# Between two attention layers: weight splits moved from VectorE and GpSimd to ScalarE and GpSimd, masked values written directly, PSUM banks taken one at a time

## The chip, the cores and the metric

The kernel runs on one core of a Trainium2 chip. The time is the device time of one execution in microseconds (us). Of the engines, TensorE (PE) multiplies matrices, VectorE (DVE), ScalarE (ACT) and GpSimd (POOL) work element by element, and SyncE (SP) issues most of the transfers. Each engine works through its own instructions in the order in which they are written; semaphores tie the engines together.

## The reference

Two layers, each `x <- x + RMSNorm_post(Mixer(RMSNorm_pre(x)))`, for 512 tokens of 1,024 columns in float32. Layer 0 is sparse attention with 16 heads in 4 groups: compressed keys and values (blocks of 32 tokens through a small network), selected blocks and a window, mixed by gates. Layer 1 is differential attention with 8 heads. Cut to what matters here:

```
u = rmsnorm(x, norm_pre[0]);  q, kc, vc, ks, vs, kw, vw, gate, z = split(u @ w_in)
o_c = softmax(q @ k_cmp + bias) @ v_cmp          # 31 compressed blocks per group
o   = gate0*o_c + gate1*o_s + gate2*o_w
x   = x + rmsnorm((o * silu(z)) @ w_out, norm_post[0])
u = rmsnorm(x, norm_pre[1]);  q, k, v, z = split(u @ dw_in)
a = softmax(q1 @ k1) - lam * softmax(q2 @ k2)    # differential attention, then a @ v
```

## The kernel before

**Splitting.** A float32 operand is split into two parts, a rounded high one (`hi`, names ending in h, whi) and the rest (`lo`, names ending in l, wlo), and a product is three matmuls: high by high, low by high, high by low. Weights are loaded (`wraw`, or for a few pieces two `P` tiles) and split piece by piece by `Stream.split`: a copy makes the high part (L163 ACT, L165 POOL, or for one piece L159), a subtraction the low part (L167, or L160). A piece listed in `ws.by` is split by the engines that a table names, two letters for each quarter: first the engine of the high part, then that of the low part (A = ScalarE, P = GpSimd, D = VectorE). `SPD` is the table of the first piece of `dv1`; its split parts lie in the tiles `wx`.

**Jobs.** A projection is a job whose function `run` yields after each step of three matmuls. Layer 0 ends with the jobs oA, oB, oC and `o1` (output projection, second half of its columns, four token tiles t = 0 to 3, matmuls at L467). Layer 1 begins with `dv0` and `dv1`, the value projections (`tjob`, matmuls at L218, results copied out at L571 by ACT). `dv0` goes token tile by token tile.

**The seam between the layers.** When a token tile of `o1` is done, its row sum of squares is taken (L453 ACT), the product with the norm's weights (L454 DVE), the inverse root (L345 ACT, L346 to L352 DVE) and the new x (`bigD`, L1052 DVE, two halves). `prenorm` then takes the sum of squares of the new x (L361 ACT), multiplies x by the next norm's weights (L364 POOL, two halves, into `bigC`), computes a root again (L345 to L349), scales `bigC` (L369 DVE, two halves) and returns `turn`: eight transposes by PE (L380) into two PSUM tiles T, whose high part ACT writes (L100, into `bigF`) and whose low part DVE writes (L105, into `bigE`). `bigF` and `bigE` are the operands of layer 1's projections. `T["pre", t]()` is the turn of tile t, called p0 to p3 here; the string `SEQ` writes the order on PE out by hand: a0 to a3 are the token tiles of `dv0` (24 matmuls each), b0 to b3 those of the first half of `dv1` (12 each).

**PSUM.** `bank(tag)` takes a bank of 128 x 512: 2 with tag mm, 2 with S, 3 with T, 1 with av. The rest of the order is set by a scheduler that simulates the program and by the pools' buffers; only PE's order in the seam is fixed.

**Compressed values.** Class `Cmp`, one for each group: `t` turns the probabilities and prepares the value operand `vt`: for each of four heads the same 64 columns, multiplied by that head's mask (`bmask`, one column each, so that rows of other heads are zero), split in two. Before, DVE writes the masked copy with one instruction (L918, into a P tile), ACT rounds it (L100) and DVE subtracts (L105 PT<-P). `v` multiplies (L931 to L933) and adds into the output (L935). L870 and L878 are the product of probabilities with values and its sum into the output.

Of the kernel before, what the change touches and what calls it, by code (L numbers as in the profile page):

```python
# [21 lines left out]
PRE1 = 29  # L22
# [20 lines left out]
SPD = ('PD',)*4  # L43
SEQ = 'a0 a1 p2 b0 b1 a2 p3 b2 a3 b3'.split()
# [24 lines left out]
def trunk(ctx: ExitStack, tc: tile.TileContext, x, table, npre, npost, w_in, pe_k, w1_k, w2_k,  # L69
# [135 lines left out]
    def tjob(name, w, width, col, n, evac, banks, cuts=((0, 4), (4, 4)), by_token=False):  # L205
        def run(i):
            bs = [bank(b) for b in banks]
            per = 4 // len(bs)
            acc = [bs[t // per][:, (t % per) * n:(t % per) * n + n] for t in range(NT)]
# [14 lines left out]
            if by_token:  # L224
                for ci in range(len(cuts)):
                    cut[ci] = ws.cut.pop(i + ci)
                for t in range(NT):
                    for ci in range(len(cuts)):
                        yield from part(ci, t)
                    evac(t, acc[t])  # L230
                for _ in cuts:
                    if i:
                        ws.split()
                return
# [120 lines left out]
    def prenorm(t, src, xn, grow, uh, ul, early):  # L355
# [6 lines left out]
        if early:  # L362
            for c, g in zip(halves, grow):
                nc.gpsimd.tensor_tensor(xn[:, c], src[:, c], g, op=OP.mult)  # L364
# [226 lines left out]
    for n in range(4):  # L591
        tjob(f"dv{n}", dw_in, DIFF_IN, 2048 + n * 256, 256, evac_dv(n), (("S", "S"), ("mm", "mm"))[n % 2],
             by_token=n == 0)
# [287 lines left out]
    class Cmp:  # L881
# [22 lines left out]
        def t(self, i):  # L904
            g = self.g
            if True:
                p = bank("T")
                for qb in range(NT):
# [7 lines left out]
                vb = ptile()  # L916
                v3 = vb[:, 0:256].rearrange("p (h d) -> p h d", h=4)
                nc.vector.tensor_tensor(v3, T["vc"][:, g:g + 1, :].to_broadcast([128, 4, 64]),  # L918
                                        bmask[:, :, None].to_broadcast([128, 4, 64]), op=OP.mult)
                vt = pttile()  # L920
                hi(vt[:, 0:256], vb[:, 0:256])
                lo(vt[:, 256:512], vb[:, 0:256], vt[:, 0:256])
# [156 lines left out]
    with tc.manual_schedule(engines={mybir.EngineType.PE}):  # L1079
        run.upto("oC")  # L1080
        while run.i <= index["o1"]:
            run.step()
            if run.done - T.setdefault("o1b", run.done) > PRE1 * 640:
                if ("pre", 1) in T:
                    T.pop(("pre", 1))()
# [4 lines left out]
        for w in SEQ:  # L1090
            if w[0] == "p":
                T["pre", int(w[1])]()
            else:
                for _ in range({"a": 8, "b": 4}[w[0]]):
                    next(gens["ab".index(w[0])], None)
        for g in gens:
            for _ in g:
                pass
# [180 lines left out]
```

## Time and profile before

| what | value |
|---|---|
| runs | 663.24, 663.30, 665.05 us; median 663.3 us |
| profiled execution, its own time | 661.7 us |
| its span, first to last instruction | 659.8 us |
| PE busy | 635.3 us of the span |
| granted TensorE clock, mean | 0.99 of full speed |

The profiled execution lies 1.6 us below the median of the others; differences are worked out against it and then taken from the median. A PE that is busy for 96% of the span leaves about 24.5 us in which it does nothing, and some of those are the start and the end.

### The profile page before, as it was taken

Reading aid. Unit: us, or ns where it says so; the run is one execution under the profiler, and the core shown is the slowest. Engines: PE = TensorE matmul, PEld = TensorE weight load, DVE = VectorE, ACT = ScalarE, POOL = GpSimd, SP = SyncE. Lnnn points to the kernel's source line nnn. Section 1 sums busy time; section 2 is a strip of 40 time slices with the busy share of each in tenths; the row PEclk is TensorE's granted clock in tenths of the full one; section 3 lists DMA queues with packets and bytes.
Section 4 is the critical chain, followed back from the end, with each engine's and each line's share of the span. In section 5 each row is a group of like instructions: output and inputs, shape, how many; then the busy total and the mean of one; then the engine's idle time right before and its main releaser. Section 6 shows DMA issues by size and latency. Waiting matters only on the chain.

```text
span 659.8 us, 11242 instructions
## 1 busy us (share of the span) xinstructions
PE 635.3 (96%) x3773; PEld 555.5 (84%) x3773; DVE 413.7 (63%) x1188; ACT 340.3 (52%) x904; POOL 401.3 (61%) x675
## 2 busy tenths in 40 slices
PE   6999999999999999999999899999999998989996
PEld 5888888888788788888887899898987987879885
DVE  5611235678778978969878900236558668797634
ACT  6311234675767567768564311235564574668431
POOL 4778558777777587768586457948674563522300
PEclk8999999999999999999999899999999998999998
DMA  8565423213022111201852212322333232225302
GB/s 254 145 166 132 124 76 92 60 34 71 27 65 66 33 47 41 58 17 36 298 187 96 96 54 75 117 74 89 88 81 79 68 80 62 65 64 191 129 25 103
DMA packets 68989, 60.52 MB, mean 92 GB/s; under 512 B 3628, under 2 KB 60868, under 8 KB 68932
## 3 DMA queue, kind: packets, MB, share of 16 engines
q1 hardware_dynamic: 68212, 57.45, 29.9%
q10 hardware_dynamic: 720, 2.36, 0.9%
q8 instruction: 30, 0.49, 0.3%
q14 instruction: 27, 0.22, 0.1%
HBM read 55.04 MB, written 4.76 MB: 91 GB/s over the span
## 4 chain that ended last, share of the span: by engine, by line
PE 81%; DVE 11%; ACT 3%; DMA 3%; issue 2%; POOL 0%; SPq 0%; DVEq 0%; ACTq 0%; POOLq 0%
PE mm L198 31%; PE mm L218 12%; PE mm L467 6%; PE T L856 5%; PE av L870 5%; PE S L218 5%; PE S L801 4%; PE S L800 4%; PE S L467 3%; PE av L1166 2%; PE T L721 1%; DMA wraw<-in_nsa_w_in_dram 1%; PE T L1156 1%; DMA P<-in_nsa_w_out_dram 1%; DVE P L792 1%
## 5 line engine op out<-in xcount | busy, mean ns | idle before, releaser
L167 POOL TENSOR_TENSOR wlo<-wraw,whi 128x256 fp32r<-128x256 f32 (+2 forms) x247 | 184.2, 774 | 23.8 <-ACT whi L163 12.4
L165 POOL TENSOR_SCALAR whi<-wraw 128x256 fp32r<-128x256 f32 (+1 forms) x240 | 95.5, 424 | 111.9 <-PE mm L198 65.9
L794 ACT ACTIVATE P<-P,st 128x512 f32<-128x512 f32 (+3 forms) x192 | 107.5, 560 | 87.6 <-DVE st L792 86.7
L850 POOL TENSOR_SCALAR P<-P,st,gate 128x512 f32<-128x512 f32 (+3 forms) x128 | 80.1, 637 | 27.0 <-DVE st L847 24.9
L792 DVE CUSTOM_DVE_ANT_0 P<-S,BT 128x128 f32<-128x128 f32 (+2 forms) x144 | 59.7, 418 | 28.6 <-PE S L801 26.1
L198 PE MATMUL mm<-bigA,whi 128*128 128x512 f32 x192 | 77.4, 403 | 0.1
L198 PE MATMUL mm<-bigA,wlo 128*128 128x512 f32 x192 | 75.3, 392 | 0.0
L198 PE MATMUL mm<-bigB,whi 128*128 128x512 f32 x192 | 75.3, 392 | 0.0
L105 DVE TENSOR_TENSOR PT<-T,PT 128x512 fp32r<-128x512 f32 x84 | 56.9, 685 | 8.2 <-ACT PT L100 6.4
L870 PE MATMUL av<-PT,bigE 128*128 128x512 f32 x160 | 56.4, 417 | 1.2 <-DVE bigF L878 0.9
L105 DVE TENSOR_TENSOR stk<-mm,stk 64x512 fp32r<-64x512 f32 x32 | 22.0, 688 | 52.5 <-ACT stk L100 52.1
L198 PE MATMUL mm<-bigF,whi 128*128 128x512 f32 x128 | 51.9, 405 | 0.0
L856 PE MATMUL T<-ident,P 128*128 128x128 f32 x320 | 51.8, 272 | 0.0
L100 ACT ACTIVATE PT<-T 128x512 fp32r<-128x512 f32 x84 | 48.6, 592 | 6.0 <-PE T L856 3.9
L856 PEld LDWEIGHTS T<-ident,P 128*128 128x128 f32 x320 | 41.0, 140 | 12.3 <-issue 0.4
L100 ACT ACTIVATE stk<-mm 64x512 fp32r<-64x512 f32 x64 | 37.8, 591 | 25.8 <-PE mm L198 14.9
L198 PE MATMUL mm<-bigE,whi 128*128 128x512 f32 x128 | 50.8, 397 | 0.0
L198 PE MATMUL mm<-bigF,wlo 128*128 128x512 f32 x128 | 50.7, 396 | 0.0
L218 PE MATMUL mm<-whi,bigF 128*128 128x256 f32 x176 | 50.3, 287 | 0.1
L218 PE MATMUL mm<-wlo,bigF 128*128 128x256 f32 x176 | 50.0, 285 | 0.0
L218 PE MATMUL mm<-whi,bigE 128*128 128x256 f32 x176 | 49.6, 283 | 0.0
L198 PEld LDWEIGHTS mm<-bigB,whi 128*128 128x128 f32 x192 | 36.1, 188 | 8.1
(288 smaller groups left out, 1650.8 us busy)
## 6 DMA issues: line engine op xcount, KB each, us to landing
wraw<-in_diff_w_in_dram SPq DMA_DIRECT2D x31, 512.0 KB, 3.9
wraw<-in_nsa_w_in_dram SPq DMA_DIRECT2D x26, 512.0 KB, 4.1
BT<-rd SPq DMA_DIRECT2D x32, 128.0 KB, 3.4
wraw<-in_diff_w_out_dram SPq DMA_DIRECT2D x5, 512.0 KB, 4.0
bigF<-in_x_dram SPq DMA_DIRECT2D x4, 512.0 KB, 9.5
wraw<-in_nsa_w_out_dram SPq DMA_DIRECT2D x4, 512.0 KB, 3.4
bigD<-in_x_dram SPq DMA_DIRECT2D x4, 512.0 KB, 3.7
x1d<-bigD ACTq DMA_DIRECT2D x4, 512.0 KB, 4.9
```

Of the source, the lines that this page charges most:

```text
L100: return nc.scalar.activation(dst, src, AF.Copy, scale=scale)
L105: nc.vector.tensor_tensor(dst, src, h.bitcast(F32), op=OP.subtract)
L165: nc.gpsimd.tensor_scalar(h[:, a:b], v, 1.0, 0.0, op0=OP.mult, op1=OP.add)
L167: e.tensor_tensor(l[:, a:b], v, h[:, a:b].bitcast(F32), op=OP.subtract)
L198: T["mm"] = nc.tensor.matmul(p[:, a:b], wt[:, k, :], u[:, k, a:b], start=(k == 0 and j == 0), stop=(k == KD - 1 and j == 2)).ins
L218: nc.tensor.matmul(acc[t], u[:, k0 + k, t * 128:(t + 1) * 128], wt[:, k, :], start=(ci == 0 and k == 0 and j == 0 and t % per == 0), stop= ...
L467: nc.tensor.matmul(p, U[u][:, k, t * 128:(t + 1) * 128], wt[wi], start=start and j == 0, stop=stop and j == 2, skip_group_check=True)
L792: nc.vector.tensor_tensor_reduce(out=o, in0=i0, in1=b, op0=OP.add, op1=OP.min, scale=-1.0, scalar=BIG, accum_out=nm)
L794: nc.scalar.activation(pt[:, :n], pt[:, :n], AF.Exp, bias=nm, scale=-1.0, accum_out=den)
L850: NORM(nc, i, br, qb).tensor_scalar(self.P[i][:, :n], self.P[i][:, :n], st[:, 8 + i:9 + i], gate[:, NT - 1 - qb, c:c + 1], op0=OP.mult, op ...
L856: T["tmark"] = nc.tensor.transpose(p[:, j * 128:(j + 1) * 128], self.P[j][:, kb * 128:(kb + 1) * 128], ident).ins
L870: nc.tensor.matmul(av, T["V"][:, br, kb, g, :], p, start=(br == 0 and kb == 0 and j == 0), stop=(br == 1 and kb == qb and j == 1))
```

## The change

Five edits, the first four at the seam. (1) The four quarters of the first piece of `dv1` get their high part from ScalarE and their low part from GpSimd, instead of GpSimd and VectorE. (2) The turn p1 is called after `o1` instead of after 29 of its steps, so behind its last three matmuls. (3) `dv0` takes a PSUM bank for each token tile when it comes to it, with the tags S, T, S, S, instead of two S banks, two token tiles in each, before it starts. (4) What the seam's block issues on POOL stays behind the last L364 instruction (`issue_after`). (5) `Cmp.t` writes no masked copy: for each head ACT writes the high part with the mask as its scale, and DVE computes value times mask minus the high part.

```
-PRE1 = 29
-SPD = ('PD',)*4
-SEQ = 'a0 a1 p2 b0 b1 a2 p3 b2 a3 b3'.split()
+SPD = ('AP',)*4
+SEQ = 'p1 a0 a1 p2 b0 b1 a2 p3 b2 a3 b3'.split()
...
-            bs = [bank(b) for b in banks]
-            per = 4 // len(bs)
-            acc = [bs[t // per][:, (t % per) * n:(t % per) * n + n] for t in range(NT)]
+            if by_token:
+                per, acc = 1, [None] * NT
+            else:
+                bs = [bank(b) for b in banks]
+                per = 4 // len(bs)
+                acc = [bs[t // per][:, (t % per) * n:(t % per) * n + n] for t in range(NT)]
...
                 for t in range(NT):
+                    acc[t] = bank(banks[t])[:, :n]
                     for ci in range(len(cuts)):
...
-                nc.gpsimd.tensor_tensor(xn[:, c], src[:, c], g, op=OP.mult)
+                T["xm"] = nc.gpsimd.tensor_tensor(xn[:, c], src[:, c], g, op=OP.mult).ins
...
-        tjob(f"dv{n}", dw_in, DIFF_IN, 2048 + n * 256, 256, evac_dv(n), (("S", "S"), ("mm", "mm"))[n % 2],
-             by_token=n == 0)
+        tjob(f"dv{n}", dw_in, DIFF_IN, 2048 + n * 256, 256, evac_dv(n),
+             (("S", "T", "S", "S"), ("mm", "mm"), ("S", "S"), ("mm", "mm"))[n], by_token=n == 0)
...
-                vb = ptile()
-                v3 = vb[:, 0:256].rearrange("p (h d) -> p h d", h=4)
-                nc.vector.tensor_tensor(v3, T["vc"][:, g:g + 1, :].to_broadcast([128, 4, 64]),
-                                        bmask[:, :, None].to_broadcast([128, 4, 64]), op=OP.mult)
                 vt = pttile()
-                hi(vt[:, 0:256], vb[:, 0:256])
-                lo(vt[:, 256:512], vb[:, 0:256], vt[:, 0:256])
+                for h in range(4):
+                    a, b, m = vt[:, 64 * h:64 * h + 64], vt[:, 256 + 64 * h:320 + 64 * h], bmask[:, h:h + 1]
+                    hi(a, T["vc"][:, g], m)
+                    nc.vector.scalar_tensor_tensor(b, T["vc"][:, g], m, a.bitcast(F32), op0=OP.mult, op1=OP.subtract)
...
-        while run.i <= index["o1"]:
-            run.step()
-            if run.done - T.setdefault("o1b", run.done) > PRE1 * 640:
-                if ("pre", 1) in T:
-                    T.pop(("pre", 1))()
+        run.upto("o1")
...
+        with tc.issue_after(T["xm"]):
+            for w in SEQ:
...
```

How the instructions stand now, at three places. The line numbers of the change differ by one to three: L159 there is L160 of before, L164 is L165, L166 is L167, L220 is L218, L351 is L348, L367 is L364, L383 is L380, L470 is L467, L795 is L792, L850 is L847 and L881 is L878; L923 is the new subtraction.

PE at the end of `o1` (tile t = 3, the S bank), before:

```order
L467 MATMUL S<-wx,bigA 128x512 x2
L467 MATMUL S<-wx,bigB 128x512
L380 MATMUL T<-ident,bigC 128x128 x8
L467 MATMUL S<-wx,bigA 128x512 x2
L467 MATMUL S<-wx,bigB 128x512
L218 MATMUL S<-whi,bigF 128x256
L218 MATMUL S<-wlo,bigF 128x256
```

and in the change:

```order
L470 MATMUL S<-wx,bigA 128x512 x2
L470 MATMUL S<-wx,bigB 128x512
L470 MATMUL S<-wx,bigA 128x512 x2
L470 MATMUL S<-wx,bigB 128x512
L383 MATMUL T<-ident,bigC 128x128 x8
L220 MATMUL S<-whi,bigF 128x256
L220 MATMUL S<-wlo,bigF 128x256
```

The eight transposes of p1 moved behind the last three matmuls of `o1`.

POOL in the seam, before; the four L364 instructions are tiles 0 and 1, then tiles 2 and 3:

```order
L364 TENSOR_TENSOR bigC<-bigD,P 128x512 x4
L165 TENSOR_SCALAR whi<-wraw 128x256 x4
L167 TENSOR_TENSOR wlo<-wraw,whi 128x256 x2
L159 TENSOR_SCALAR wx<-P 128x256 x4
L167 TENSOR_TENSOR wlo<-wraw,whi 128x256 x2
L364 TENSOR_TENSOR bigC<-bigD,P 128x512 x4
L165 TENSOR_SCALAR whi<-wraw 128x256 x4
```

and in the change:

```order
L367 TENSOR_TENSOR bigC<-bigD,P 128x512 x4
L159 TENSOR_TENSOR wx<-P,wx 128x256 x4
L367 TENSOR_TENSOR bigC<-bigD,P 128x512 x4
L164 TENSOR_SCALAR whi<-wraw 128x256 x4
L166 TENSOR_TENSOR wlo<-wraw,whi 128x256 x4
L164 TENSOR_SCALAR whi<-wraw 128x256 x4
```

Between tiles 1 and 2 four subtractions stand where twelve instructions stood; eight of those (the second piece of `dv1`) went behind tile 3, and the four copies (before's L159) went to ACT, where they stand ahead of tile 2's L361.

DVE around the compressed values of the second group, before:

```order
L792 ISA st 128x1
L918 TENSOR_TENSOR P<-vcmp,bmask 128x256
L878 TENSOR_TENSOR bigF<-av,PT 64x2x128 x2
L105 TENSOR_TENSOR PT<-T,PT 128x512
L792 ISA P,st<-S,BT_78 128x512
```

and in the change, some ten rows further on:

```order
L850 RECIPROCAL st<-st 128x2
L104 TENSOR_TENSOR PT<-T,PT 128x512
L923 SCALAR_TENSOR_TENSOR PT<-vcmp,bmask,PT 128x64 x4
L795 ISA P,st<-S,BT_78 128x512
L795 ISA st 128x1
L881 TENSOR_TENSOR bigF<-av,PT 64x2x128 x2
```

The masked product is gone from in front of the sum L878, and four small subtractions stand where one of 256 columns stood.

## Rows read from the trace of the kernel before

**Rows 1.** The page's first part: busy us, share of the span, instructions of each engine.
```profile
PE 635.3 (96%) x3773; PEld 555.5 (84%) x3773; DVE 413.7 (63%) x1188; ACT 340.3 (52%) x904; POOL 401.3 (61%) x675
```
**Rows 2.** Waits of PE over the span: us in total, times, longest.
```profile
PE av L870 <- DVE bigF L878: 0.9, 1, 0.9
```
**Rows 3.** Timeline of PE: start, duration (us), instruction, [idle before <- releaser].
```profile
359.02 0.39 PE L467 MATMUL S<-wx,bigB 128*128 128x512 f32 x1
...
362.42 1.25 PE L380 MATMUL T<-ident,bigC 128*128 128x128 f32 x8 [0.97 <-DVE bigC L369]
363.43 0.71 PE L467 MATMUL S<-wx,bigA 128*128 128x512 f32 x2
...
364.21 0.28 PE L218 MATMUL S<-whi,bigF 128*128 128x256 f32 x1
...
366.97 0.28 PE L218 MATMUL S<-whi,bigE 128*128 128x256 f32 x1
369.69 0.58 PE L218 MATMUL S<-whi,bigF 128*128 128x256 f32 x1 [2.44 <-ACT bigA L571]
...
374.09 1.04 PE L380 MATMUL T<-ident,bigC 128*128 128x128 f32 x8
```
**Rows 4.** Timeline of DVE in the same stretch.
```profile
357.24 1.25 DVE L346 SCALAR_TENSOR_TENSOR rs<-ss,m 128x1 f32<-128x1 f32 x1 [0.88 <-ACT PT L361]
...
360.47 0.89 DVE L348 SCALAR_TENSOR_TENSOR rs<-rstd,rs 128x1 f32<-128x1 f32 x2
...
361.54 1.37 DVE L369 TENSOR_SCALAR bigC<-bigC,rstd,rs 128x512 f32<-128x512 f32 x2
...
365.47 3.26 DVE L160 TENSOR_TENSOR wx<-P,wx 128x256 fp32r<-128x256 f32 x3
...
369.05 1.27 DVE L105 TENSOR_TENSOR bigE<-T,bigF 128x512 fp32r<-128x512 f32 x2
...
372.68 1.41 DVE L1052 SCALAR_TENSOR_TENSOR bigD<-bigC,rstd,bigD 128x512 f32<-128x512 f32 x2
```
**Rows 5.** Timeline of POOL in the same stretch.
```profile
355.50 2.97 POOL L364 TENSOR_TENSOR bigC<-bigD,P 128x512 f32<-128x512 f32 x2 [3.50 <-DVE bigD L1052]
...
359.91 1.44 POOL L167 TENSOR_TENSOR wlo<-wraw,whi 128x256 fp32r<-128x256 f32 x2
...
364.96 3.15 POOL L364 TENSOR_TENSOR bigC<-bigD,P 128x512 f32<-128x512 f32 x2
```
**Rows 6.** Timeline of ACT: its last instruction before 364.43.
```profile
358.82 0.29 ACT L345 ACTIVATE rstd<-ss,m 128x1 f32<-128x1 f32 x1
```
**Rows 7.** Timelines of DVE and POOL at the second group's masked product.
```profile
214.45 3.14 DVE L918 TENSOR_TENSOR P<-vcmp,bmask 128x256 f32<-128x256 f32 x1
...
214.25 0.73 POOL L167 TENSOR_TENSOR wlo<-wraw,whi 128x256 fp32r<-128x256 f32 x1
...
215.17 2.13 POOL L167 TENSOR_TENSOR wlo<-wraw,whi 128x256 fp32r<-128x256 f32 x3
```
**Rows 8.** Groups by form: count | busy us, mean ns | idle before.
```profile
L1189 DVE SCALAR_TENSOR_TENSOR PT<-PT,drs,bigB 128x128 f32<-128x128 f32 x32 | 8.7, 346 | 0.0
...
L105 DVE TENSOR_TENSOR PT<-P,PT 128x256 fp32r<-128x256 f32 x4 | 1.7, 418 | 0.3 <-ACT PT L100 0.3
...
L100 ACT ACTIVATE PT<-P 128x256 fp32r<-128x256 f32 x4 | 1.6, 409 | 1.3 <-PE av L870 1.3
```
**Rows 9.** Waits of PE's weight loads from 320 to 420 us.
```profile
PEld mm L467 <- DVE m L335: 0.3, 1, 0.3
PEld mm L467 <- DVE bigB L105: 0.3, 1, 0.3
```
**Rows 10.** PE behind two other gaps; busy times by stretch (sixth: granted clock).
```profile
550.25 0.64 PE L800 MATMUL S<-stk 128*128 128x512 f32 x1 [1.92 <-DVE stk L421]
...
588.83 0.50 PE L800 MATMUL S<-stk 128*128 128x512 f32 x1 [1.90 <-DVE stk L421]
...
370.00:373.00 3.00, 3.00 (x15) 3.00 (x15) 3.00 (x14) 0.00 (x0) 0.00 (x0) 0.51 0.00 1
```

More of the change, by code (lines that the diff above doesn't have):

```diff
@@ L1089, in trunk @@
         gens = [jobs[index[n]].run(jobs[index[n]].first) for n in ("dv0", "dv1")]
[L1090 to L1098, printed above, removed]
+        with tc.issue_after(T["xm"]):
+            for w in SEQ:
+                if w[0] == "p":
+                    T["pre", int(w[1])]()
+                else:
+                    for _ in range({"a": 8, "b": 4}[w[0]]):
+                        next(gens["ab".index(w[0])], None)
+            for g in gens:
+                for _ in g:
+                    pass
         run.i = index["dv2"]
```

## The prediction

> **What bounds the kernel now.** I read the page first: PE is busy for 635.3 of 659.8 us [rows 1]. The change adds and removes no matmul, so all it can give is some of the 24.5 us in which PE stands, and time in which PE runs at a lower clock. I then asked which of PE's waits lie where the change works. In the timeline of PE at the seam there are two: 0.97 us before the transposes of p1, for the scaling L369 of tile 1, and 2.44 us before the second token tile of `dv0` [rows 3]. After the second the 24 matmuls of that tile take 4.4 us (369.69 to 374.09), where the 24 of the first took 2.9 (364.21 to 366.97 and one more step of 0.12): the granted clock was 0.51 from 370 to 373, the level of 1.2 GHz [rows 3, 10]. So the seam holds 3.4 us of standing and 1.5 us of slow clock. The compressed values hold one wait: 0.9 us behind the sum L878 [rows 2]. Just before the seam the weight loads waited twice 0.3 us for DVE [rows 9]. The most that the change can return is about 3.4 + 1.5 + 0.9 + 0.6 = 6.4 us.
>
> The 2.44 us carries ACT's name, the copy of `dv0`'s first tile out of the bank that the second shares. That copy isn't alone: the low part of tile 1 (two L105 from 369.05, 1.27 us) was half done at 369.69 too [rows 3, 4]. The third matmul of the token tile reads it. It was late because four L160 stood ahead of it on DVE, the first three for 3.26 us while POOL ran L364 [rows 4, 5]. A new bank alone would therefore give back almost nothing.
>
> **What DVE and POOL do to each other.** This decides the seam. L346, of one column, takes 1.25 us and ends at 358.49; POOL's two L364 end at 358.47 [rows 4, 5]. The pair of L348, also of one column, starts at 360.47 and is held for most of 0.89 us, until about 361.3, where POOL's two L167 end [rows 4, 5]. A DVE instruction with two operands in SBUF stands while POOL subtracts or multiplies. The masked product L918 shows how long: it starts at 214.45 and takes 3.14 us, through one L167, a gap of 0.2 us and three more L167 that end at 217.30 [rows 7]. It didn't get in between two POOL instructions that followed each other.
>
> **The change part by part.**
>
> *Masked copy (edit 5).* L918 goes. In the second group it stood ahead of L878, and PE waited 0.9 us for that sum [rows 2, 7]. With nothing ahead of it but its own operands, this wait goes: **-0.9 us**, bounds 0 and -0.9. In return ACT gets four instructions of 64 columns for one of 256 (0.41 us), and DVE four for one (0.42) [rows 8]. On DVE one costs at most the 0.35 us of a 128-column one of the same kind, so four take 0.4 to 1.4 us; I take 0.9, since 64 columns lie below that row. The first subtraction can follow the first copy, so the last is done about as late as now: zero for the path. These small ones have two SBUF operands, so they can be held as L918 was; a rival below.
>
> *The end of layer 0.* Without L918 and with another order of ACT's pieces, the splits ahead of `o1` are done earlier on DVE; the two waits of 0.3 us [rows 9] are bounded by 0 and 0.6. I take **-0.4**.
>
> *p1 behind `o1` (edit 2).* The three matmuls between 363.43 and 364.21 run before PE waits: 0.8 us of work ahead of the wait instead of behind it, a gain if p1 is ready no later than now.
>
> *Splits (edit 1).* It is ready later. ACT is free at 359.1 [rows 6], but the buffer `wx` is read by PE until 359.4 (359.02 and 0.39) [rows 3]. The first copy ends at about 359.8 (0.41, rows 8's price for 256 columns). From then POOL runs four L160 at L167's price, 1.44 / 2 = 0.72 each [rows 5]: to 362.7. The pair of L348 arrives at 360.47 and is held until then, 1.4 us longer than before. From its end at 361.36 to the first half of L369 done before p1 (362.42) it took 1.06, with POOL in the way; free of POOL I allow 0.8, so p1 starts at 363.5. PE finishes `o1` at 361.45 + 0.8 = 362.2 in the counting of its starts, and stands 1.3 us. Transposes take 1.0 (362.42 to 363.43): 364.5. `dv0`'s first tile: 364.5 to 367.4.
>
> What DVE does then: second half of L369 to 364.0, the new x of tile 2 (two L1052, 1.41 [rows 4]) to about 365.6. Its first half lets POOL start L364 at 365.0, as it did at 364.96, and run 2.97 us to 368.0 [rows 5]. L346 of tile 2 now stands ahead of tile 1's low part, where the L160 stood, and is held until 368.0, as at 358.49. Then L454 and the first L105, 512 columns each (0.64, half of 1.27 [rows 4]): 369.3 to 369.4. So the wait for the low part stays, shorter by the L160 and longer by L346. The third matmul of the second token tile starts at 369.4; before, from 369.69 at full clock, at 369.93. **-0.5 us** for edits 1, 2 and 4 together, bounds -3.4 (nothing held) and +1.5 (each step half a microsecond later).
>
> *Banks (edit 3).* With a bank of its own, the first two matmuls of the second tile need only `bigF`. PE's gap is thus in two parts, some 0.5 and 1.5 us, with two matmuls between, and none is as long as 2.44. *The clock.* After 1.92 us at 550 the next matmul took 0.64 us; after 1.90 us at 588 one of the same shape took 0.50 [rows 10], so the first gap cost the clock and the second didn't. Gaps of 1.3 and 1.5 us lie under both, so I forecast that the clock stays at 2.4 GHz: **-1.5 us**, bounds 0 and -1.5.
>
> *Moved splits (edit 4).* The second piece of `dv1` is now split behind tile 3's L364, 8 instructions of at most 0.72 us: 5.8. Before, that L364 could begin after the first half of the pair of L1052 at 372.68 and took 3 us, to about 376.5; so the piece is ready by 382.3 [rows 4, 5]. PE wants it after b3: from p2, now at about 372.4, 96 matmuls of 0.12 and two rounds of transposes of 1.0 are 13.5 us, to 385.9. Zero; without that cover each microsecond of lateness is one on PE.
>
> Sum: -0.9 - 0.4 - 0.5 - 1.5 = **-3.3 us**. The profiled execution would go from 661.7 to 658.4. That one stands 1.6 us under the median of the runs, 663.3, so the forecast is 663.3 - 3.3 = **660.0 us**.
>
> **The rivals.** About 0.3% (2 us) is what a measurement here can tell from no change.
>
> *POOL lets go between instructions (chance 0.15).* If L348 gets in at the end of the L160 it meets, its pair is through by about 361.3, as before, p1 runs at 362.4 and everything behind it, L364 of tile 2 included, is 1.0 us earlier: **659.0**. The Trainium skill, page "SBUF — State Buffer", section "Who interferes with whom", says that whoever issues first gets the shared pair "for the whole instruction", which by itself would hand it over at each end; L918's 3.14 us, through several POOL instructions, disagree.
>
> *The clock falls again (0.22).* The two gaps with two matmuls between add up to 2 us, as long as the one at 550. Then 1.5 us aren't returned: **661.5**. For it: nearly equal gaps at 550 and 588 came out differently.
>
> *The waits move (0.13).* The scheduler has set the whole order of layer 0 anew from the first group on; the 0.9 us wait may reappear at the next sum, and the clock may fall: only 0.5 remains, **662.8**.
>
> *Slower: the small subtractions meet a run of POOL (0.12).* L932 needs them. If in two of four groups they stand behind a run like that of rows 7 (2.7 us lost, 3.14 less 0.42), PE loses up to 5.4 us; less the seam's 2.0 and the 0.9: 663.3 + 2.5 = **665.8**. It decides from about one such meeting on. Against it: the subtraction L105 PT<-P, which stood at that place with two such operands, took 0.42 us in the mean of four [rows 8], so it was held in none.
>
> **How the numbers follow.** My forecast has 0.38. Its own range is 659.0 to 661.0, half a microsecond for each of two sized terms. The range 657.8 to 663.2 takes in handing over with the whole of the 0.6, the fallen clock and the moved waits, and leaves out most of the slower case. Faster by over 0.3% (below 661.3): 0.38 + 0.15 and 0.05 of the fallen clock, 0.58. The same: 0.17 + 0.13 = 0.30. Slower: 0.12.
>
> **What would show it.** Right: no wait of PE behind L878 near 218; L348 of tile 1 held for about 2 us, until POOL's fourth L160 ends; PE waiting for p1 1 to 1.5 us and again inside the second token tile, whose 24 matmuls run at a granted clock near 1.0; L346 of tile 2 ending with L364. Wrong: L348 short, or the clock at 0.5 after the seam, or DVE's four L923 taking over 1.5 us in a group with PE waiting for them. A wait of PE for the second piece of `dv1` would refute the cover of edit 4.

## The result and the profile after

| | before | changed |
|---|---|---|
| median, first measurement | 663.27 us (4 runs) | 656.57 us (4 runs: 655.58 to 657.36) |
| ratio, 95% interval | | 0.9893 [0.987, 0.9917] |
| profiled execution, its span | 661.7, 659.8 us | 655.58, 653.8 us |
| median, second measurement | 662.04 us (27 runs) | 658.66 us (10 runs: 656.09 to 660.93) |
| ratio, 95% interval | | 0.994 [0.9914, 0.9965] |

The change is faster, by 6.7 us in the first measurement, twice the 3.3 forecast and below the forecast range of 657.8 to 663.2, and by 3.4 in the second. Single runs of one kernel spread over 5 to 7 us there, and part of the document is about what varies. Line numbers of the changed kernel are one to three off those of before, as listed at the orders above.

**Where the profiled 6.0 us of span come from.** Every matmul has its counterpart in the other trace, so the lead can be read at each: 0.2 us up to the attention stage; in layer 0's attention it rises by 1.9, at the end of layer 0 it falls by 0.4, in the seam it rises by 3.0, and by 1.3 at one gap of layer 1 near 546, where nothing was changed; 0.1 comes later. The 1.9 is itself a net: the lead rises by 2.8 to 265 of the kernel before and falls back by 0.9 in the third group. A part of that is seen as a wait of PE's weight load there (0.2 us before):

```profile
PEld S L932 <- DVE st L795: 0.5, 1, 0.5
```

The page's first part, answering to [rows 1]:

```profile
span 653.8 us, 11276 instructions
...
PE 632.9 (97%) x3773; PEld 553.5 (85%) x3773; DVE 406.3 (62%) x1192; ACT 344.3 (53%) x920; POOL 403.7 (62%) x675
```

PE's timeline in the seam of the changed kernel (start, duration, instruction; in brackets the wait before it), answering to [rows 3]:

```profile
354.82 0.48 PE L470 MATMUL S<-whi,bigA 128*128 128x512 f32 x1
...
360.64 0.66 PE L383 MATMUL T<-ident,bigC 128*128 128x128 f32 x4
361.59 0.63 PE L383 MATMUL T<-ident,bigC 128*128 128x128 f32 x4 [0.30 <-DVE rstd L355]
361.98 0.36 PE L220 MATMUL S<-whi,bigF 128*128 128x256 f32 x1
...
365.21 0.38 PE L220 MATMUL T<-whi,bigF 128*128 128x256 f32 x1
...
366.71 0.38 PE L220 MATMUL T<-whi,bigE 128*128 128x256 f32 x1 [1.00 <-DVE bigE L104]
...
369.44 1.04 PE L383 MATMUL T<-ident,bigC 128*128 128x128 f32 x8
370.24 0.48 PE L220 MATMUL mm<-wx,bigF 128*128 128x256 f32 x2
```

The wait of 1.3 us that was forecast ahead of p1 isn't there; that of 1.5 inside the second token tile is 1.0, at the third matmul and behind DVE's low part, as described. The clock, answering to [rows 10] (busy time, matmuls, granted clock, share of DMA, GB/s):

```profile
365.00:370.00 5.00, 3.87 (x31) 1.00 0.02 7
370.00:373.00 3.00, 3.00 (x28) 1.00 0.45 180
```

It stayed at 2.4 GHz, where it was at 0.51 before. DVE in the same stretch, answering to [rows 4], and POOL, to [rows 5]:

```profile
358.80 0.82 DVE L351 SCALAR_TENSOR_TENSOR rs<-rstd,rs 128x1 f32<-128x1 f32 x2
...
359.79 1.66 DVE L372 TENSOR_SCALAR bigC<-bigC,rstd,rs 128x512 f32<-128x512 f32 x2
...
361.55 1.41 DVE L1053 SCALAR_TENSOR_TENSOR bigD<-bigC,rstd,bigD 128x512 f32<-128x512 f32 x2
...
364.13 1.26 DVE L349 SCALAR_TENSOR_TENSOR rs<-ss,m 128x1 f32<-128x1 f32 x1 [0.88 <-ACT PT L364]
365.31 0.68 DVE L457 TENSOR_TENSOR bigC<-S,P 128x512 f32<-128x512 f32 x1
...
365.98 1.28 DVE L104 TENSOR_TENSOR bigE<-T,bigF 128x512 fp32r<-128x512 f32 x2
```

```profile
358.15 3.01 POOL L159 TENSOR_TENSOR wx<-P,wx 128x256 fp32r<-128x256 f32 x4 [1.29 <-ACT wx L99]
362.38 2.99 POOL L367 TENSOR_TENSOR bigC<-bigD,P 128x512 f32<-128x512 f32 x2 [1.22 <-DVE bigD L1053]
```

The pair L351 (L348 of before) took 0.82 us while POOL's four low parts ran for 3.01. A narrower piece of the two timelines parts the pair: its second instruction is held from 358.92 to 359.62, and the second of POOL's four ends at 359.60.

```profile
358.92 0.70 DVE L351 SCALAR_TENSOR_TENSOR rs<-rstd,rs 128x1 f32<-128x1 f32 x1
```

```profile
358.86 0.74 POOL L159 TENSOR_TENSOR wx<-P,wx 128x256 fp32r<-128x256 f32 x1
```

The first of the pair took 0.20 us and was hardly held. The second waits for the one POOL instruction that it meets, and gets in while two more are still to come. The same view of before shows L348's second one from 360.59 to 361.36, and POOL's second L167 ending at 361.34. The merged row of [rows 4] hid that. And it was no exception: in the trace of before, 31 DVE instructions took 0.3 us or more longer than the shortest of their kind and saw a POOL instruction end meanwhile. For 29 of them it was one; only two, the masked copies L918 of the first and second group, were held through several. This is one of the 29 (here the first of a pair), inside a run of four L167 from 492.61 to 495.44:

```profile
494.20 0.57 DVE L1182 TENSOR_TENSOR dss<-dss,drr 128x8 f32<-128x8 f32 x1
```

```profile
494.00 0.74 POOL L167 TENSOR_TENSOR wlo<-wraw,whi 128x256 fp32r<-128x256 f32 x1
```

### The profile page after: what moved, and what is told of

Its sections match the earlier page's. It is cut to its first block, busy times and chain, and to the rows that moved or that the text cites. A ratio compares the mean times of both kernels' runs of the same rounds, so it can differ in the third digit from the quotient of the medians.

```text
span 653.8 us, 11276 instructions
## 1 busy us (share of the span) xinstructions
PE 632.9 (97%) x3773; PEld 553.5 (85%) x3773; DVE 406.3 (62%) x1192; ACT 344.3 (53%) x920; POOL 403.7 (62%) x675
## 4 chain that ended last, share of the span: by engine, by line
PE 83%; DVE 9%; DMA 3%; ACT 2%; issue 1%; SPq 0%; DVEq 0%; ACTq 0%
PE mm L197 31%; PE mm L220 12%; PE mm L470 6%; PE av L873 5%; PE T L859 5%; PE S L804 4%; PE S L803 4%; PE S L220 4%; PE S L470 3%; PE av L1164 2%; PE T L724 1%; DMA P<-in_nsa_w_out_dram 1%; PE T L1154 1%; DMA P<-in_diff_w_in_dram 1%; DMA wraw<-in_nsa_w_in_dram 1%
## 5 line engine op out<-in xcount | busy, mean ns | idle before, releaser
L166 POOL TENSOR_TENSOR wlo<-wraw,whi 128x256 fp32r<-128x256 f32 (+2 forms) x247 | 184.2, 775 | 23.2 <-DVE drr L1144 11.4
L164 POOL TENSOR_SCALAR whi<-wraw 128x256 fp32r<-128x256 f32 (+1 forms) x240 | 97.4, 432 | 103.4 <-PE mm L197 61.5
L795 DVE CUSTOM_DVE_ANT_0 P<-S,BT 128x128 f32<-128x128 f32 (+2 forms) x144 | 59.7, 418 | 28.1 <-PE S L804 25.6
L104 DVE TENSOR_TENSOR PT<-T,PT 128x512 fp32r<-128x512 f32 x84 | 56.9, 685 | 7.2 <-ACT PT L99 5.0
L104 DVE TENSOR_TENSOR stk<-mm,stk 64x512 fp32r<-64x512 f32 x32 | 22.0, 689 | 52.2 <-ACT stk L99 51.8
L220 PE MATMUL mm<-whi,bigF 128*128 128x256 f32 x176 | 50.3, 287 | 0.1
L220 PE MATMUL mm<-wlo,bigF 128*128 128x256 f32 x176 | 50.0, 285 | 0.0
L220 PE MATMUL mm<-whi,bigE 128*128 128x256 f32 x176 | 49.6, 283 | 0.0
```

The costliest lines, as they stand in the source:

```text
L104: nc.vector.tensor_tensor(dst, src, h.bitcast(F32), op=OP.subtract)
L164: nc.gpsimd.tensor_scalar(h[:, a:b], v, 1.0, 0.0, op0=OP.mult, op1=OP.add)
L166: e.tensor_tensor(l[:, a:b], v, h[:, a:b].bitcast(F32), op=OP.subtract)
L220: nc.tensor.matmul(acc[t], u[:, k0 + k, t * 128:(t + 1) * 128], wt[:, k, :], start=(ci == 0 and k == 0 and j == 0 and t % per == 0), stop= ...
L795: nc.vector.tensor_tensor_reduce(out=o, in0=i0, in1=b, op0=OP.add, op1=OP.min, scale=-1.0, scalar=BIG, accum_out=nm)
```

## The experiments

The measure for the seam is the stretch on PE from the first matmul of `o1`'s last token tile to the first of b0. The same matmuls lie between in every kernel. Before it is 374.88 - 356.43 = 18.45 us, in the changed kernel 370.24 - 354.82 = 15.42. It repeats within 0.1 us where the same kernel was profiled twice, so it tells more than times do. The ratio comes with its interval from the single runs and can differ from the quotient of the two medians by some tenths of a per cent.

| kernel | edits | seam us | waits of PE in it | median us (of before) | ratio, 95% interval |
|---|---|---|---|---|---|
| before | none | 18.45 | 1.0, 2.4, slow clock | 663.27 | |
| before again | none | 18.38 | 1.0, 2.4, slow clock | 663.30 (662.04) | 1.001 [0.9989, 1.0031] |
| changed | 1 to 5 | 15.42 | 0.3, 1.0 | 656.57 (663.27) | 0.9893 [0.987, 0.9917] |
| changed again | 1 to 5 | 15.41 | 0.3, 1.0 | 658.66 (662.04) | 0.994 [0.9914, 0.9965] |
| values alone | 5 | 18.55 | 1.0, 2.4, slow clock | 660.81 (662.28) | 0.9988 [0.9972, 1.0004] |
| seam alone | 1 to 4 | 15.43 | 0.3, 1.0 | 658.25 (662.28) | 0.9956 [0.9936, 0.9976] |
| splits undone | 2 to 5 | 13.68 | 0.5 | 656.74 (662.04) | 0.9903 [0.9868, 0.9938] |
| p1's place undone | 1, 3 to 5 | 14.48 | 0.8, 0.3 | 655.39 (661.71) | 0.9896 [0.9877, 0.9914] |
| banks undone | 1, 2, 4, 5 | 15.42 | 0.3, 1.2 | 657.54 (662.28) | 0.994 [0.9916, 0.9963] |
| order undone | 1 to 3, 5 | 19.67 | 0.3, 0.3, 1.6, 1.0, slow clock | 661.56 (662.04) | 0.9975 [0.9951, 0.9998] |
| splits and order undone | 2, 3, 5 | 19.02 | 0.3, 1.2, 2.2, slow clock | 662.14 (661.71) | 1.0007 [0.9992, 1.0021] |
| order alone | 4 | 14.59 | 0.3, 0.8 | 658.69 (662.12) | 0.9946 [0.9928, 0.9963] |
| two long subtractions | 1 to 5 | 16.52 | 1.6, 1.0 | 657.30 (662.28) | 0.9933 [0.991, 0.9956] |
| quarters | 2 to 5 | 12.96 | none | 655.20 (661.71) | 0.9891 [0.987, 0.9913] |
| order, values, quarters | 4, 5 | 13.78 | 0.6 | 656.28 (662.12) | 0.991 [0.9891, 0.9929] |

**The two halves of the change.** Edit 5 alone, and edits 1 to 4 alone (the old `Cmp.t` in the changed kernel):

> The kernel before with edit 5 alone (the masked values written directly). Theory A, read from the two traces: the masked copy L918 was held behind POOL's subtractions (3.14 us at 214.45, 2.15 us at 160.26), and with it go four waits of PE in the attention stage of layer 0, 0.22 + 0.91 + 0.23 + 0.20 us and a little around them, 1.9 us in all: about 661.4 against 663.3, ratio 0.997. Theory B, the prediction: only the 0.9 us behind L878 and 0.4 at the end of layer 0 go, 662.0, ratio 0.998. Either way no wait of PE behind the sum L878 near 218, and the end of layer 0 tells whether the 0.44 us that the change lost there come from this edit.

> The changed kernel with the old masked copy, so edits 1 to 4 alone. Theory A: the seam gives 3.0 us by itself (1.5 of standing, 1.5 of clock): 660.2, ratio 0.9954, and the wait of 0.9 us behind L878 is back. Theory B, the prediction's terms: 0.5 and 1.5 us, 661.3, ratio 0.997. If the profiled gain of 1.3 us at the gap near 546 belongs to the change and not to chance, this run has it too, or the run with edit 5 alone has it.

The seam's 3.0 us belong to edits 1 to 4 (15.43), and edit 5 leaves the seam alone (18.55). With edit 5 the wait of 0.9 us behind the sum is gone; against the profile of before it gains 1.9 us in layer 0's attention (a rise of 2.8 and a fall of 0.9, as above) and loses 0.5 at its end, 1.4 net. The median says 1.5, with an interval that holds no change. The run of the seam alone has a surprise: without edit 5 it too gains 1.3 us between 150 and 168. Its first masked copy (L921 there, L918 of before) wasn't held:

```profile
160.69 0.68 DVE L921 TENSOR_TENSOR P<-vcmp,bmask 128x256 f32<-128x256 f32 x1
```

```profile
161.07 0.91 POOL L166 TENSOR_TENSOR wlo<-wraw,whi 128x256 fp32r<-128x256 f32 x1
```

The copy came 0.38 us ahead of POOL's subtraction, which then took 0.91 instead of 0.73: this time POOL waited. In before and its repeat the copy came 0.36 and 0.37 us ahead and was held, so hundredths of a microsecond lie between the outcomes; what tips them isn't shown.

**Two long subtractions.** POOL's four low parts of 256 columns as two of 512:

```
+            if i in self.by and i > 1:
+                for a in range(0, n, 2):
+                    for k in range(a, a + 2):
+                        hi(h[:, k:k + 1], raw(k, k + 1))
+                    nc.gpsimd.tensor_tensor(l[:, a:a + 2], raw(a, a + 2), h[:, a:a + 2].bitcast(F32), op=OP.subtract)
...
```

> The changed kernel with the four subtractions of POOL for the first piece of dv1 (256 columns, about 0.74 us each) made as two of 512 columns (about 1.45 us each); nothing else moves on any engine. Theory A (a DVE instruction with operands in SBUF waits to the end of the one POOL instruction that it meets, then gets in): the two L351 of tile 1 are held by one long instruction each, until about 360.0 and 361.4 instead of 359.0 and 359.6; the scaling L372 is free of POOL behind that, p1 starts at about 362.1 instead of 360.6, and the kernel is 1.1 us slower (0.8 to 1.5), 657.7. Rival (the pair is held for the whole run of POOL whatever its pieces, the prediction's step): the run lasts as long as before, so nothing moves, within 0.2 us of 656.6.

```profile
359.01 1.94 DVE L358 SCALAR_TENSOR_TENSOR rs<-rstd,rs 128x1 f32<-128x1 f32 x2
```

```profile
358.41 2.53 POOL L156 TENSOR_TENSOR wx<-P,wx 128x512 fp32r<-128x512 f32 x2 [1.33 <-ACT wx L99]
```

POOL's run is shorter in all (2.53 us against 3.01), and yet the pair is held for 1.94 us instead of 0.82, each by one long instruction. The seam grew by 1.10 us, the expected 1.1. In the seam the length of POOL's single instruction sets the price, not that of its run.

**One edit undone at a time.** Edit 3 (two S banks taken before `dv0` starts), edit 1, edit 4, and edit 2 (p1 after 29 steps of `o1`), each from the changed kernel with the lines of before put back:

```
-(("S", "T", "S", "S"), ("mm", "mm"), ("S", "S"), ("mm", "mm"))[n]
+(("S", "S"), ("mm", "mm"))[n % 2]
...
-SPD = ('AP',)*4
+SPD = ('PD',)*4
...
-        with tc.issue_after(T["xm"]):
+        if True:
...
-SEQ = 'p1 a0 a1 p2 b0 b1 a2 p3 b2 a3 b3'.split()
+SEQ = 'a0 a1 p2 b0 b1 a2 p3 b2 a3 b3'.split()
```

> The changed kernel with edit 3 undone: dv0 takes two S banks at its start, two token tiles in each. Theory A (the bank splits PE's gap and so keeps the clock): PE stands once for about 2.5 us ahead of the second token tile (365.2 to 367.7, where the low part of tile 1 comes), the granted clock falls to about 0.5 behind it, and the kernel loses 0.2 us for the two matmuls that filled the gap and about 1.5 us for the clock: +1.7 us, 658.3. Rival (the clock's fall before was chance, or the bank is only a wait): +0.2 us with the clock at 1.0, or more than 2 us if the copy out of the first tile comes later than the low part.

> The changed kernel with edit 1 undone: POOL makes the high parts of the first piece of dv1, DVE the low ones, four instructions ahead of the new x of tile 2. Theory A (edit 1 is what gives the seam its 1.5 us of standing, since it takes 4 x 0.41 = 1.65 us of DVE out of the way): POOL's multiplication of tile 2 and with it p2 come about 1.0 us later (1.65 less the 0.7 that the pair L351 was held, and p2 has 0.55 us of slack: scaled at 368.89, begun at 369.44), and PE stands at p2 instead of ahead of the third matmul of the second token tile: 0.5 to 1.7 us slower at a full clock, up to 1.5 more where the clock falls: about 657.6. Rival (another order of DVE's work is the source): within 0.3 us of the changed kernel.

> The changed kernel with edit 4 undone: the scheduler then puts eight splitting instructions of a later piece (L164 x4, L166 x4) ahead of or among the four low parts of the first piece of dv1, and all of them ahead of POOL's multiplication of tile 2. Theory A (edit 4 is needed as soon as edit 1 puts the low parts on POOL): POOL is busy until about 366.5 instead of 361.2, the multiplication starts 2.4 us later than at 364.08 (tile 2's first half), p2 has 0.55 us of slack, so about 2 us slower (1 to 3), 658.6, and 1.5 more if the clock falls in the gap. Rival (the prediction's zero for edit 4): within 0.3 us.

> The changed kernel with edit 2 undone: p1 goes ahead of the last three matmuls of o1. Theory A (edit 2 is worth the work that covers the wait): PE stands some 0.7 us ahead of p1 and dv0 starts 0.65 us later, but DVE then makes tile 1's low part (L104) ahead of the held L349 of tile 2, so the wait of 1.0 us inside the second token tile goes and p2 comes later instead (it has 0.55 us of slack): the seam gives about 2.5 us instead of 3.0, bounds 2.1 and 3.3. Rival, the prediction's price: 0.8 us less, with the wait inside the second token tile still there.

*Banks undone:* the seam is the same to 0.01 us. PE stands once, for 1.25 us behind ACT's copy, and the clock stays. So beside edits 1 and 2 edit 3 gives nothing in this profile, neither by its bank nor by the clock.

*Splits undone:* the seam is 1.74 us shorter, against both expectations. Beside the other edits, edit 1 is a loss. DVE in this kernel:

```profile
361.54 1.00 DVE L372 TENSOR_SCALAR bigC<-bigC,rstd,rs 128x512 f32<-128x512 f32 x2
362.46 0.42 DVE L159 TENSOR_TENSOR wx<-P,wx 128x256 fp32r<-128x256 f32 x1
...
362.87 1.09 DVE L159 TENSOR_TENSOR wx<-P,wx 128x256 fp32r<-128x256 f32 x3
363.87 1.40 DVE L1053 SCALAR_TENSOR_TENSOR bigD<-bigC,rstd,bigD 128x512 f32<-128x512 f32 x2
365.20 0.68 DVE L104 TENSOR_TENSOR bigE<-T,bigF 128x512 fp32r<-128x512 f32 x1
...
365.89 0.69 DVE L104 TENSOR_TENSOR bigE<-T,bigF 128x512 fp32r<-128x512 f32 x1
366.50 1.22 DVE L349 SCALAR_TENSOR_TENSOR rs<-ss,m 128x1 f32<-128x1 f32 x1
```

The four subtractions cost DVE 1.5 us and nothing holds them, POOL being idle then. And the scheduler now puts tile 1's low part (L104) ahead of the held L349, so PE goes through the second token tile without standing; only 0.5 us remain ahead of p2.

*Order undone:* 4.25 us longer, of which PE's slow clock is a part (0.91 over 340 to 375). POOL:

```profile
358.05 1.52 POOL L164 TENSOR_SCALAR whi<-wraw 128x256 fp32r<-128x256 f32 x4
359.54 2.14 POOL L166 TENSOR_TENSOR wlo<-wraw,whi 128x256 fp32r<-128x256 f32 x3
361.62 0.92 POOL L159 TENSOR_TENSOR wx<-P,wx 128x256 fp32r<-128x256 f32 x1
362.51 0.91 POOL L166 TENSOR_TENSOR wlo<-wraw,whi 128x256 fp32r<-128x256 f32 x1
363.37 3.03 POOL L159 TENSOR_TENSOR wx<-P,wx 128x256 fp32r<-128x256 f32 x3
366.36 1.27 POOL L367 TENSOR_TENSOR bigC<-bigD,P 128x512 f32<-128x512 f32 x1
```

Eight instructions of a later piece stand ahead of tile 2's multiplication. It starts 10.3 us after the seam's first matmul, and 7.6 us after it in the changed kernel.

*p1's place undone:* 0.94 us shorter, so edit 2 is a loss beside the others, outside my bounds. PE stands 0.8 us ahead of p1 as expected, but here too the low part goes ahead of the held L349, and p2 doesn't come later.

**Edit 4 with and without company.** Edits 1 and 4 undone, and edit 4 alone in the kernel before:

> The changed kernel with edits 1 and 4 undone, so edits 2, 3 and 5: POOL splits the later piece (L164 x4, L166 x4) around the copies of the first piece of dv1, all ahead of its multiplication of tile 2, and DVE makes tile 1's low part behind the held L349 again. With edit 4 alone kept the seam gave 4.8 us against the profile of before. Theory A (edit 4 is the source of the gain, by its order on POOL): here the seam gives 1.5 to 2.5 us, with a wait of 1.5 to 2 us inside the second token tile, and less if the clock falls there. Rival (edits 2 and 3 are the source): over 4 us again.

> The kernel before with edit 4 alone: POOL makes the eight splitting instructions of the later piece (L165, L167) behind its last multiplication by the norm's weights, instead of ahead of tile 2's. Theory A (edit 4 is the source): without L165 and L167 in the way POOL's multiplication of tile 2 starts as soon as its first half of x is there, and DVE isn't held by L167: the seam gives 4 to 5 us against before and the clock stays at 1.00 from 340 to 375; about 658 against the 662 of before on this chip, ratio 0.993 to 0.994. Rival (edit 4 needs p1 behind o1 or the banks of edit 3): under 2 us.

Edit 4 alone gives 3.9 us of the seam, more than all four together; edits 2 and 3 without it lengthen the seam by 0.6, where a gain of 1.5 to 2.5 was expected. It is the source. How it works is seen on DVE and POOL of the kernel with edit 4 alone:

```profile
362.35 1.09 DVE L160 TENSOR_TENSOR wx<-P,wx 128x256 fp32r<-128x256 f32 x3
...
364.68 1.28 DVE L105 TENSOR_TENSOR bigE<-T,bigF 128x512 fp32r<-128x512 f32 x2
```

```profile
364.19 2.96 POOL L364 TENSOR_TENSOR bigC<-bigD,P 128x512 f32<-128x512 f32 x2 [3.47 <-DVE bigD L1052]
```

DVE's L160 now stand ahead of tile 2's new x, while POOL is idle, and three of them take 1.09 us instead of the 3.26 of [rows 4]. Tile 1's low part starts 8.3 us after the seam's first matmul, before 12.6. Some of the gain is the clock, which stayed at 1.00 here: against a seam of before at full clock (17.0 us, seen in two variants of it below) edit 4 alone gives 2.4 us, and the whole change 1.6.

**A version that gains more.** Edits 2 to 5 with POOL's multiplication L367 in quarters of 256 columns, and the same with edits 4 and 5 alone:

```
-            for c, g in zip(halves, grow):
-                T["xm"] = nc.gpsimd.tensor_tensor(xn[:, c], src[:, c], g, op=OP.mult).ins
+            for c, g in zip(halves, grow):
+                for k in (0, 256):
+                    d = slice(c.start + k, c.start + k + 256)
+                    T["xm"] = nc.gpsimd.tensor_tensor(xn[:, d], src[:, d], g[:, k:k + 256], op=OP.mult).ins
```

> The changed kernel with edit 1 undone, and POOL's multiplication by the norm's weights made in quarters of 256 columns instead of halves of 512; nothing else moves on any engine. Theory A (a DVE instruction waits to the end of the one POOL instruction that it meets): L349 of tile 2, held for 1.22 us until the half ended, is held for at most 0.75, and the 0.5 us that PE stood ahead of p2 go: 0.5 us less than with edit 1 undone alone, 656.2. Rival (it waits for POOL's whole run): no change, or some tenths more for the added instructions on POOL.

> The kernel before with edits 4 and 5, and POOL's multiplication by the norm's weights in quarters of 256 columns. Theory A: the seam gives 5 us or more, PE's waits there go but for the 0.3 to 1 us ahead of p1 (it is called before the last three matmuls of o1), and edit 5 adds what it gave alone: about 655 to 656, ratio 0.989 to 0.99, the same as with edits 2 to 5 and quarters (0.9891). Rival: p1 ahead of the last matmuls costs what edit 2 was to give, 0.8 us more.

```profile
340.00:375.00 35.00, 35.00 (x213) 1.00 0.25 91
```

That is the window over the seam of the first of these two kernels: PE doesn't stand in it at all. With 12.96 us its seam is 2.5 us shorter than the changed kernel's. Its ratio of 0.9891 is below the second measurement of the changed kernel (0.994) and equals the first; the two weren't timed side by side, so that the whole kernel is faster than the changed one is not shown by the times. The second kernel's seam gave 4.7 us where 5 or more was expected: PE still waits 0.6 us there for ACT's copy out of the bank that two token tiles share. With the low part early, a bank for each token tile may thus be worth something after all; no run has edit 3 as its only difference there.

**What varies.** The changed kernel and the one before, each once more:

> The changed kernel once more, unaltered, for another profile on the chip of the other runs. Theory A (the 1.3 us that the profiled run of the change gained at the gap near 546 are chance of the clock): the matmul after that gap may take 0.64 us again and the granted clock from 540 to 570 be 0.94 instead of 1.00, with a span near 655.1; the seam gives its 3.0 us either way, at a clock of 1.00. Rival (the gain belongs to the change): clock 1.00 from 540 to 570 and a span near 653.8 again.

> The kernel before once more, unaltered. Theory A: the masked copy of the first group, held for 2.15 us at 160.26, is a near miss of some tenths with POOL's subtractions (it took 0.68 us in the run with the seam's edits alone, where it began 0.37 us ahead of L167): here it may take either, and with it come or go 1.2 us; the one of the second group is held for 3.1 us again, with a wait of PE of 0.9 us. The seam shows a single gap of 2.4 us and the granted clock near 0.5 behind it. Rival (every one of these is fixed by the program): 2.15 and 3.14 us again.

The seam is 15.41 and 18.38 us, again 3.0 apart. In the repeat of before, the first masked copy was held for 3.03 us at 160.93 instead of 2.15, and PE waited behind L878 twice, 1.9 us in all. With 0.68 in the run of the seam alone, that copy is a near miss: it took 0.68, 2.15 and 3.03 us. The long one:

```profile
160.93 3.03 DVE L918 TENSOR_TENSOR P<-vcmp,bmask 128x256 f32<-128x256 f32 x1
```

The clock varies too. Behind the gap of 1.93 us near 546, which no edit touches, the mean granted clock of 540 to 570 was 0.94 in 11 of the 18 profiles and 1.00 in 7, the changed kernel's two among these (before, and then after):

```profile
550.25 0.64 PE L800 MATMUL S<-stk 128*128 128x512 f32 x1 [1.92 <-DVE stk L421]
```

```profile
545.66 0.50 PE L803 MATMUL S<-stk 128*128 128x512 f32 x1 [1.93 <-DVE stk L424]
```

The repeat of the change, which ran at 1.00 there as well, had only 0.9 us less lead than the first, all of it lost before 100 us. Theory and rival of that run aren't told apart by it alone; the runs of splits, p1's place and order undone (1.00) and of banks and seam alone (0.94) show both clocks with most edits in place, so I take the 1.3 us for chance, although before showed 0.94 and the changed kernel 1.00 in both of its two profiles. That the clock varies within one kernel is on record in the single runs: of the ten of the changed kernel in the second measurement, the five with a mean granted clock of 0.992 or more took 656.1 to 657.8 us, and the five with 0.989 or less 659.5 to 660.9. The 27 of before beside them go from 659.9 to 660.6 at 0.995 to 663.5 to 666.7 at 0.985. In these two sets most of the spread between runs goes with the clock.

**Why the masked copy was held so long.** Three variants of the kernel before: the copy made by four instructions of 64 columns; a one-column product of two mask columns, overwritten by the copy, at the copy's place, with the copy one or two instructions later; and the same of two columns of the identity.

```
+                for h in range(4):
+                    nc.vector.tensor_scalar(vb[:, 64 * h:64 * h + 64], T["vc"][:, g], bmask[:, h:h + 1], None, op0=OP.mult)
...
+                nc.vector.tensor_tensor(vb[:, 0:1], bmask[:, 0:1], bmask[:, 1:2], op=OP.mult)
...
+                nc.vector.tensor_tensor(vb[:, 0:1], ident[:, 0:1], ident[:, 1:2], op=OP.mult)
```

> The kernel before, with the masked copy made by four DVE instructions of 64 columns (value times a mask column as a scalar) instead of one of 256 with two operands spread over heads. In the second group three of them stand where L918 was held for 3.14 us behind four subtractions of POOL. Theory A (one POOL instruction for each DVE instruction that meets it): they end at the ends of the first three subtractions, 215.0, 215.9 and 216.6, and the sum L878 starts near 216.7 instead of 217.5, so PE's wait of 0.9 us shrinks to about 0.1. Theory B (whatever stands there is held through the whole run): 217.5 and 0.9 us as before. Theory C (the new form isn't held at all): four times 0.2 us, the sum near 215.3, no wait. The time is 0 to 1 us under that of before.

> The kernel before with one more DVE instruction, a product of two columns of the mask (one column, two operands in SBUF), at the place where the masked copy L918 was held; the copy itself stands one or two instructions later. Theory A (the place: what comes first behind the row maxima L792 is held through POOL's run): the one-column instruction takes 2 to 3 us in the groups near 161 and 216, up to the end of POOL's run. Theory B (the length: a short one slips in at the end of the POOL instruction that it meets, a long one doesn't): at most 0.8 us there, and the copy behind it is held for long where it meets a run.

> As the run with the one-column product ahead of the masked copy, with two columns of the identity matrix as operands instead of two of the mask. Theory A (the stretch of layer 0, whatever is read there): held for 1.9 and 2.9 us again in the groups near 160 and 215, to the end of POOL's run. Theory B (the mask's tile as an operand): at most 0.8 us, to the end of the one POOL instruction that it meets; the masked copy behind it may still be held in the third group.

The first took 664.83 us against 661.71 (1.0044 [1.0026, 1.0061]), where 0 to 1 us less was expected; in its profile 1.9 us are lost around the third group, where the four pieces took 2.67 us and the single copy of before 0.44. The others, one run each, took 662.16 and 665.27. DVE with the one-column product, and POOL beside it:

```profile
214.62 2.88 DVE L917 TENSOR_TENSOR P<-bmask 128x1 f32<-128x1 f32 x1
...
270.36 2.63 DVE L919 TENSOR_TENSOR P<-vcmp,bmask 128x256 f32<-128x256 f32 x1
```

```profile
214.43 0.73 POOL L167 TENSOR_TENSOR wlo<-wraw,whi 128x256 fp32r<-128x256 f32 x1
215.10 0.29 POOL L649 COPY BC<-BT 128x64 f32<-128x64 f32 x1
215.35 2.13 POOL L167 TENSOR_TENSOR wlo<-wraw,whi 128x256 fp32r<-128x256 f32 x3
```

One column was held through the whole run to 217.48, and so it was with the identity as operand (2.90 us at 216.01). Of the four pieces, the first was held for 2.91 us in the second group, while in the third group three that followed each other took 0.8 us each and got in between POOL's instructions. Length, form and operand are thus not the reason, and the place isn't either, since the copy at 270.36, behind other work, was held too. In all 18 traces only this copy, its first piece or the one-column product ahead of it were ever held through several POOL instructions, 15 times; none was after edit 5. Why these go through several and all others through one stays open.

## Why the prediction was wrong

**The step that failed** is "The pair of L348 arrives at 360.47 and is held until then, 1.4 us longer than before", until the end of POOL's fourth subtraction. It was held for 0.82 us, through the second. All that followed in my chain is 1.0 to 1.3 us early by it: tile 2's new x was done at 362.96, in the counting of before (1.6 us more) 364.6 and not 365.6, the third matmul ran at 368.3 and not 369.4. This is the rival "POOL lets go between instructions", place and price: it asked for 0.5 + 1.0 + 1.5 = 3.0 us from the seam, and the seam gave 3.03. The two long subtractions show its mechanism. What misled me was one instruction, the masked copy of [rows 7], which behaves otherwise than the 29 others held in the same trace. I also read its "gap of 0.2 us" wrongly: POOL's copy L649 runs there, so it was held through five POOL instructions:

```profile
214.92 0.29 POOL L649 COPY BC<-BT 128x64 f32<-128x64 f32 x1
```

The rival's price has luck in it, since 1.5 us of it are the clock (below). The sentence of the Trainium skill, page "SBUF — State Buffer", section "Who interferes with whom", "for the whole instruction", agrees with the seam's rows (L351 until 359.62, POOL until 359.60) and with POOL's 0.91 us when DVE came first; layer 0's 2.88 us for one column isn't what it says.

**Point by point.**

- *Masked copy, -0.9:* the wait behind L878 is gone, but the profile gained 1.9. I priced the second group alone; the first one's copy was held too (2.15 us). The first group gave about 1.0, which is the near miss that came and went with the runs, the second about 1.6, and the third took 0.9 back. The four L923 were free, 0.28 us each, 1.1 in all against the 0.9 assumed, and none was held in a trace (0.28 to 0.29 at most in the changed kernel): the slower rival didn't come.
- *End of layer 0, -0.4:* the sign was wrong, it cost 0.44, and 0.5 in the run of edit 5 alone. The weight load of the first product with the values, L932, waits 0.6 us for ACT's small pieces (L931 waited 0.5 before), and the splits for `o1` aren't earlier. That this is where the 0.4 us come from isn't shown. The weight loads' waits there, answering to [rows 9]:

```profile
PEld T L932 <- ACT PT L99: 0.6, 1, 0.6
PEld mm L470 <- DVE bigB L104: 0.6, 2, 0.4
```

- *Edits 1, 2 and 4 together, -0.5:* measured -1.5 with edit 3. The sum hid that they pull apart: from the changed kernel, edit 1 costs 1.74, edit 2 costs 0.94 and edit 4 gives 4.25. I priced edit 4 by the piece that it makes late (zero, and no wait of PE for dv1's second piece appeared), not by what stands in the way without it. Alone it takes DVE's subtractions out of POOL's way and brings the low part of tile 1 forward by 4.3 us.
- *The low part of tile 1 behind the held L346 of tile 2:* right, 1.00 us at the third matmul. It is also what edits 1 and 2 cost, since with either undone the scheduler puts it ahead.
- *Banks, clock, -1.5:* the clock did stay, but not by edit 3: a single gap of 1.25 us kept it as well. And the price was half chance: behind the gap of 2.4 us in the seam of before the clock fell in four profiles (before, its repeat, edit 5 alone, the identity probe) and stayed at 1.00 in two (the copy in four, the mask probe), whose seams are 17.03 and 17.02 us, 1.4 shorter.
- *The sum:* of the profiled 6.0 us, 3.0 are the seam, 1.9 - 0.4 layer 0, 1.3 the clock near 546, 0.2 the start and the end. So of the 2.7 us beyond the forecast the failed step accounts for 1.0, layer 0 for 0.2, where two errors nearly cancel, and the clock near 546 for 1.3. The range had no place for a gap outside the change that came out otherwise. The medians were 6.7 us apart in the first measurement, of four runs each, and 3.4 in the second. The near miss and the gaps of the clock, each worth some 1.3 us in a run, are large enough for that difference, and the median of the second lies between the runs at a higher and at a lower clock. That its 3.4 us are next to the forecast 3.3 is luck: the steps behind the 3.3 were wrong as told here. Which of the two medians is nearer to the truth, the runs don't settle.

## What to carry to other kernels

Before a DVE instruction is priced against a run of POOL, read the two timelines instruction by instruction; a merged row and one long example decide nothing. POOL's work that nobody needs soon, put ahead of work on the path, was most of the seam's loss (3.9 of the 5.5 us found), so order it first, and then cut POOL's single instructions short where DVE's small ones meet them. Undo edits one at a time even when the sum is a gain: two of the four took back a part of what one gave. And look at the clock of the single runs before two medians are compared.

## What was not expected of the hardware

A DVE instruction of one column with two operands in SBUF took 0.19 us free, 0.70 us across one POOL instruction in the seam, and 2.88 us across a run of four POOL subtractions and a copy in layer 0. The same gap of PE (2.44 us, and 1.93) was followed by about half the clock (0.51 and 0.53) in some executions and by 1.00 in others.
